# One forward step of a hybrid backbone: another order of instructions in the odd layer

## The chip, the cores and the metric

The kernel runs on one core of one Trainium2 chip. The time is device microseconds of an execution, as the median of several runs. The chip's engines are TensorE (PE), VectorE (DVE), ScalarE (ACT), GpSimd (POOL) and SyncE (SP), which here issues all DMAs. Each engine runs its own instructions in the order in which they were written, and waits on semaphores where one needs another's result.

## The reference, cut to what matters

Two groups of tokens (128 context tokens and 256 latent tokens, each 1024 wide) go through two layers. Layer 0 has a Fourier mixer and attention as its mixer, layer 1 (the odd layer) an RG-LRU and a bidirectional Mamba-2 SSD. A SwiGLU network follows each mixer. All is float32. The mixer of the odd layer, shortened:

```python
p = h @ w_in
g, xl, z, xbc, dt = split(p)
xc = centred_dwconv(xl)                       # RG-LRU, 4 tiles of 128 channels
y_lru = (scan_forward(xc) + scan_backward(xc)) * gelu(g)
xs, B, C = split(silu(centred_dwconv(xbc)))   # SSD: 16 heads of 64
acs = cumsum(dt * A)                          # per direction, chunks of 128
decay = exp(where(causal, acs_q - acs_k, -inf))
y = sum_k (C_q . B_k) * decay * dt_k * xs_k + C_q * exp(acs_q) @ state_in
y_ssd = rmsnorm((y_forward + y_backward + d * xs) * silu(z))
out = concat(y_lru, y_ssd) @ w_out
```

## The kernel before, in words

Activations stand with channels on the partitions and 386 columns: 128 context tokens, two extra columns for the modulation, 256 latent tokens. Weights come in blocks of 128 by 128, eight to a DMA of 512 KB (tile `wr`). ScalarE and VectorE split each chunk into a high and a low part (`wh`, `wl`), the activations likewise (`xh`, `xl`; `mh`, `ml`; `gh`, `gl`), and `mm3` (L620) adds three products for each block. A tile of 128 outputs is so 24 products of 386 columns for the input projection, in one of 8 PSUM banks (tag `ps`).

`odd_mixer` (L1108) runs over 27 such tiles in the order of `names` (L1111): dt0 bc0 bc1 z0 xs0 z1 together, then xs1 xs2 z2 z3 xs3 xl0 z4 xs4 xs5 xl1 z5 xl2 xs6 xs7 xl3 z6 z7 g0 g1 g2 g3. What is done with a tile is recorded right behind it. `xs_tile` (L1337) convolves, transposes and weighs two heads' channels; after every second xs tile `states` (L1367) makes state products and `ssd` (L1388) is recorded twice, for two heads each. So there are four stages of four heads, behind xs1, xs3, xs5 and xs7. For a head `ssd` does the following:

- for each direction d, in rows 64d to 64d + 63: one product of 384 columns (`ps<-rr,pick`) and three of 128 columns (`ps<-pick,rr`) in a bank of the direction's own;
- a product with the identity over all rows (`ps<-mask,identr`) that adds the causal mask, then Exp on ScalarE into a tile `M`; VectorE adds the two directions and multiplies by C.B;
- one product of 64 rows for the incoming states (`ps<-ee,sel`), which VectorE multiplies into `exs`;
- for the two heads of a call together, the output in one bank, each head in 64 of the array's columns (`ps<-M,xt`, `ps<-exs,Hc`).

The shapes of array that a product takes are called forms here: (rows, columns), each rounded up to 32, 64 or 128. A projection or mask product has the form (128, 128), the directions' products (64, 128), head outputs and state products (128, 64).

No engine's order is written by hand. `Recorder.add` (L230) notes every operation with its place `seq` in the program, its dependences and the buffers that it takes. `Recorder.schedule` (L307) then plans them one by one against a model of the engines' times and emits them in the order of their planned starts. For each engine it looks at the ready operations, takes the earliest start, and among those that can start by then the one with the lowest place. For TensorE, `quarter` holds when each part of the array is free; a product can start when the parts of its `groups` are. How the model decides depends on which part of the program holds the oldest open operation: 0 the first mixer, 1 its SwiGLU, 2 `odd_mixer`, 3 the second SwiGLU. `PARTS` (L213) has six numbers for each:

1. `window`: an operation that takes a buffer may be this many places ahead of the oldest open one;
2. `keep` and 3. `close`: of the 70 SBUF slots (tag `s`), an operation `gap` places ahead must leave more than min(1, gap / close) x keep free (L362);
4. `pad`: microseconds added between another engine's result and the TensorE operation that uses it (L449);
5. `hold`: background loads give way to other work that starts within this time;
6. `forms`: None, or the number of places by which a TensorE operation of another form than the last is put back. With a number, operations that can start within 2 x 0.105 us of the first are compared, and a change of form waits until all parts of the array are free, and `DRAIN` (0.105 us) more (L369 to L389).

Of the kernel before, what the change touches and what calls it, by code (L numbers as in the profile page):

```python
# [181 lines left out]
def meet(a, b):  # L182
    return all(x[0] < y[1] and y[0] < x[1] for x, y in zip(a, b))
# [16 lines left out]
class Recorder:  # L200
# [12 lines left out]
    PARTS = (  # L213
        (900, 10, 150, 0.8, 0.25, 60),
        (500, 12, 150, 0.4, 0.15, None),
        (900, 6, 120, 0.8, 0.25, None),
        (500, 12, 150, 0.4, 0.15, None),
    )

# [10 lines left out]
    def add(self, eng, cost, outs, ins, fn, func=None, tail=0.0, cols=0.0):  # L230
        o = Op()
        o.seq, o.eng, o.cost, o.fn, o.func, o.tail = len(self.ops), eng, cost, fn, func, tail
        o.prio = o.seq + self.base
        o.far = self.base >= self.FAR
        o.chain, o.part = self.chain, self.part
        o.cols, o.groups = cols, (0, 1, 2, 3)
        if eng == "PE":
            a, b = outs[0].box[0]
            o.groups = range(a // 32, -(-b // 32))
            k, n = ins[0].shape[0], outs[0].shape[0]  # L240
            o.form = tuple(32 if v <= 32 else 64 if v <= 64 else 128 for v in (k, n))
        if o.chain is not None:
            o.chain[0] += 1
        deps = {}
        tiles = set()
        o.allocs = []
        for v in ins:
            if not isinstance(v, Vw):
                continue
            t = v.t  # L250
            tiles.add(t)
            assert t.live, t.name
            for w, box in t.writes:
                if t.psum or meet(box, v.box):
                    deps[w] = True
            if t.psum:

                for r, box in t.reads:
                    if r.eng != eng:
                        deps[r] = True  # L260
            t.reads.append((o, v.box))
        for v in outs:
            if not isinstance(v, Vw):
                continue
            t = v.t
            tiles.add(t)
            if not t.live:
                t.live = True
                t.first = None
                if t.tag is None:  # L270
                    self.fixed.append(t)
                else:
                    t.first = o
                    o.allocs.append(t)
            elif t.first is not None and t.first is not o:
                deps[t.first] = True
            for w, box in t.writes:
                if t.psum or meet(box, v.box):
                    deps[w] = True
            keep = []  # L280
            for r, box in t.reads:
                if r is not o and (t.psum or meet(box, v.box)):
                    deps[r] = True
                else:
                    keep.append((r, box))
            t.reads = keep
            inside = lambda b: all(y[0] <= x[0] and x[1] <= y[1] for x, y in zip(b, v.box))
            t.writes = [(w, b) for w, b in t.writes if not (w is not o and inside(b))] if not t.psum else []
            t.writes.append((o, v.box))
        if o.far and eng == "SP" and self.after is not None:  # L290
            deps[self.after] = True
        if self.gate is not None:
            deps[self.gate] = True
        deps.pop(o, None)
        o.deps = list(deps)
        o.users = []
        for d in o.deps:
            d.users.append(o)
        o.n = len(o.deps)
        o.est = 0.0  # L300
        o.tiles = tiles
        for t in tiles:
            t.left += 1
        self.ops.append(o)
        return o

    def schedule(self):  # L307
# [6 lines left out]
        table = [None]  # L314
        dma_free = [0.0]

        ticks, quarter = {}, [0.0] * 4
        form = [None]
        order = []

        def avail(o):

            t = 0.0
            need = {}
            for a in o.allocs:
                if a.tag is not None:
                    need[a.tag] = need.get(a.tag, 0) + 1
            for tag, n in need.items():
                s = slots[tag]
                if len(s) < n:  # L330
                    return None
                t = max(t, heapq.nsmallest(n, s)[-1])
            return t
# [15 lines left out]
        while left:  # L349
# [5 lines left out]
            for e in engines:  # L355
                cand = []
                for o in ready[e]:
# [7 lines left out]
                    a = avail(o) if o.allocs else 0.0  # L365
                    if a is None:
                        continue
                    if e == "PE":
                        if forms is None or o.form == form[0]:  # L369
                            a = max(a, *(quarter[g] for g in o.groups))  # L370
                        else:
                            a = max(a, max(quarter) + self.DRAIN)
# [3 lines left out]
                    if e == "SP":  # L376

                        a = max(a, dma_free[0] - self.AHEAD)
# [21 lines left out]
            _, s, o = best  # L400
# [11 lines left out]
            else:  # L412
                if e == "PE":
# [3 lines left out]
                    while todo > 1e-9:  # L417
                        i = int(now / self.TICK + 1e-9)
                        c = cost if ticks.get(i - 1, 0.0) >= 3060 else 2 * cost
# [1288 lines left out]
```

## Time and profile before

| What | Before |
|---|---|
| median of 3 runs | 1012.6 us (1011.65 to 1015.13) |
| profiled execution | 1011.14 us, its span 1009.4 us |
| mean granted TensorE clock | 0.976 of full |
| busy: PE, PEld, DVE, ACT, POOL | 985.2, 932.4, 733.7, 503.4, 4.3 us |
| DMA queue q1 | 158.84 MB, 45.1% of 16 engines' span |
| stretch of the odd mixer after its first tiles | 494 to about 754 us (it holds the next SwiGLU's first products too) |

Times in the rows are microseconds from the start of the span. PE is TensorE's matmuls, PEld its weight loads. `ps<-xh,wh` is a product into PSUM of operands xh and wh; 64*128 after MATMUL are the rows and columns of the array that it uses, 64x384 the moving operand. PEclk is the clock that TensorE was granted, as a share of 2.4 GHz; an instruction's name with x6 stands for six in a row. An interval in square brackets is idle time before an instruction and what ended it. A float32 product that isn't split takes two instructions.

### The profile page before, as it was taken

Reading aid. Unit: us, or ns where it says so; the run is one execution under the profiler, and the core shown is the slowest. Engines: PE = TensorE matmul, PEld = TensorE weight load, DVE = VectorE, ACT = ScalarE, POOL = GpSimd, SP = SyncE. Lnnn points to the kernel's source line nnn. Section 1 sums busy time; section 2 is a strip of 40 time slices with the busy share of each in tenths; the row PEclk is TensorE's granted clock in tenths of the full one; section 3 lists DMA queues with packets and bytes.
Section 4 is the critical chain, followed back from the end, with each engine's and each line's share of the span. In section 5 each row is a group of like instructions: output and inputs, shape, how many; then the busy total and the mean of one; then the engine's idle time right before and its main releaser. Section 6 shows DMA issues by size and latency. Waiting matters only on the chain.

```text
span 1009.4 us, 16165 instructions
## 1 busy us (share of the span) xinstructions
PE 985.2 (98%) x6190; PEld 932.4 (92%) x6190; DVE 733.7 (73%) x1550; ACT 503.4 (50%) x951; POOL 4.3 (0%) x41
## 2 busy tenths in 40 slices
PE   6999999999999999999999899999999999999998
PEld 4987889999999999999977778899999999999998
DVE  4589666999999999984696778776889555553342
ACT  4578866343333433443496759673635333333221
POOL 0000000000000000000000000000000000000000
PEclk9999999999999999999996979899999999999999
DMA  9983426755666668643220112133463333333340
GB/s 359 368 307 110 150 85 221 256 188 196 225 213 223 215 229 259 209 148 129 89 84 11 63 47 84 48 114 130 155 251 124 125 119 120 120 122 127 125 163 24
DMA packets 47179, 159.85 MB, mean 158 GB/s; under 512 B 5376, under 2 KB 9216, under 8 KB 47104
## 3 DMA queue, kind: packets, MB, share of 16 engines
q1 hardware_dynamic: 47104, 158.84, 45.1%
q8 instruction: 48, 0.79, 0.3%
q14 instruction: 27, 0.22, 0.1%
HBM read 156.45 MB, written 2.37 MB: 157 GB/s over the span
## 4 chain that ended last, share of the span: by engine, by line
PE 91%; ACT 5%; DMA 2%; issue 1%; DVE 1%; SPq 0%; DVEq 0%; ACTq 0%
PE ps L588 89%; DMA ar<-in_ada 2%; PE ps L592 2%; ACT L528 1%; ACT kk L528 1%; SPq L581 0%; ACT ex L528 0%; ACT kl L528 0%; ACT qq L528 0%; ACT wh L528 0%; ACT M L528 0%; ACT pT L528 0%; ACT t L528 0%; ACT th L528 0%; ACT rstd L528 0%
## 5 line engine op out<-in xcount | busy, mean ns | idle before, releaser
L528 ACT ACTIVATE wh<-wr 128x1024 fp32r<-128x1024 f32 x191 | 202.0, 1058 | 360.1 <-PE ps L588 249.4
L588 PE MATMUL ps<-xh,wh 128*128 128x386 f32 x1016 | 349.5, 345 | 2.2 <-ACT rstd L528 2.2
L588 PE MATMUL ps<-xl,wh 128*128 128x386 f32 x1016 | 349.4, 344 | 0.0
L588 PE MATMUL ps<-xh,wl 128*128 128x386 f32 x1016 | 347.4, 342 | 0.0
L538 DVE TENSOR_TENSOR wl<-wr,wh 128x1024 fp32r<-128x1024 f32 x191 | 233.2, 1221 | 111.6 <-ACT wh L528 108.1
L588 PEld LDWEIGHTS ps<-xh,wh 128*128 128x128 f32 x1016 | 193.4, 191 | 6.3 <-ACT rstd L528 2.8
L588 PEld LDWEIGHTS ps<-xl,wh 128*128 128x128 f32 x1016 | 193.4, 190 | 4.2 <-issue 3.4
L588 PEld LDWEIGHTS ps<-xh,wl 128*128 128x128 f32 x1016 | 193.7, 191 | 0.9 <-issue 0.5
L551 DVE SCALAR_TENSOR_TENSOR junk<-ar,scb 128x1024 bf16<-128x1024 f32 x112 | 136.5, 1219 | 2.8 <-DMA ar<-in_ada 2.2
L588 PE MATMUL ps<-gl,wh 128*128 128x384 f32 x352 | 118.6, 337 | 0.0
L588 PE MATMUL ps<-gh,wl 128*128 128x384 f32 x352 | 118.6, 337 | 0.0
L588 PE MATMUL ps<-gh,wh 128*128 128x384 f32 x352 | 118.6, 337 | 0.0
L538 DVE TENSOR_TENSOR ft<-ps,rstd 128x386 f32<-128x386 f32 x88 | 48.3, 558 | 53.0 <-PE ps L588 50.9
L588 PEld LDWEIGHTS ps<-gl,wh 128*128 128x128 f32 x352 | 66.2, 188 | 0.0
L588 PEld LDWEIGHTS ps<-gh,wl 128*128 128x128 f32 x352 | 66.1, 188 | 0.0
L588 PEld LDWEIGHTS ps<-gh,wh 128*128 128x128 f32 x352 | 66.1, 188 | 0.0
L588 PE MATMUL ps<-ml,wh 128*128 128x384 f32 x160 | 54.3, 339 | 0.0
L588 PE MATMUL ps<-mh,wh 128*128 128x384 f32 x160 | 54.2, 339 | 0.0
L588 PE MATMUL ps<-mh,wl 128*128 128x384 f32 x160 | 53.3, 337 | 0.0
L528 ACT ACTIVATE xh<-x,G 128x128 fp32r<-128x128 f32 x64 | 26.3, 445 | 23.7 <-DVE x L551 16.7
L551 DVE SCALAR_TENSOR_TENSOR fs<-ft,fs 128x128 f32<-128x128 f32 x88 | 33.3, 414 | 4.0 <-ACT wh L528 0.5
L528 ACT ACTIVATE gh<-fs 128x384 fp32r<-128x384 f32 x44 | 23.1, 525 | 26.2 <-DVE fs L551 26.0
(226 smaller groups left out, 1082.5 us busy)
## 6 DMA issues: line engine op xcount, KB each, us to landing
wr<-in_wst SPq DMA_DIRECT2D x191, 512.0 KB, 3.3
ar<-in_ada SPq DMA_DIRECT2D x96, 512.0 KB, 4.7
x<-in_x SPq DMA_DIRECT2D x4, 386.0 KB, 9.7
out_y<-x SPq DMA_DIRECT2D x8, 193.0 KB, 2.8
scb<-in_cond SPq DMA_DIRECT2D x2, 512.0 KB, 6.6
lw<-in_lru_w SPq DMA_DIRECT2D x2, 512.0 KB, 4.6
Hc<-in_h SPq DMA_DIRECT2D x2, 256.0 KB, 4.8
out_new_ssd<-news SPq DMA_DIRECT2D x4, 128.0 KB, 1.8
```

The source lines that it names most:

```text
L528: lambda: nc.scalar.activation(out=R(out), in_=R(in_), func=func, bias=R(bias), scale=R(scale), accum_out=R(accum_out)),
L538: self.dve(out, [a, b], out.free, lambda: nc.vector.tensor_tensor(out=R(out), in0=R(a), in1=R(b), op=op))
L551: lambda: nc.vector.scalar_tensor_tensor(out=R(out), in0=R(a), scalar=R(s), in1=R(b), op0=op0, op1=op1, accum_out=R(accum_out)),
L588: self.rec.add("PE", c / 1e3, [out], [lhsT, rhs], lambda: nc.tensor.matmul(R(out), R(lhsT), R(rhs), start=start, stop=stop), cols=cols)
L592: self.rec.add("PE", 0.109, [out], [in_, ident], lambda: nc.tensor.transpose(R(out), R(in_), R(ident)), cols=2 * in_.shape[0])
```

## The change

Three places. The numbers of part 2 become (900, 10, 150, 0.4, 0.25, 200): ten slots held back with a distance of 150 instead of six with 120, a pad of 0.4 us instead of 0.8, and forms weighed with 200 places instead of not at all. The model of the array has 16 groups, four of rows by four of columns, where it had four of columns; a product takes those of the rows of its stationary operand and the columns of its output. No operation is added, removed or altered; buffers and their numbers are the same.

```diff
     PARTS = (
         (900, 10, 150, 0.8, 0.25, 60),
         (500, 12, 150, 0.4, 0.15, None),
-        (900, 6, 120, 0.8, 0.25, None),
+        (900, 10, 150, 0.4, 0.25, 200),
         (500, 12, 150, 0.4, 0.15, None),
     )
...
-        o.cols, o.groups = cols, (0, 1, 2, 3)
+        o.cols, o.groups = cols, range(16)
         if eng == "PE":
             a, b = outs[0].box[0]
-            o.groups = range(a // 32, -(-b // 32))
+            c, d = ins[0].box[0]
+            o.groups = [r * 4 + g for r in range(c // 32, -(-d // 32)) for g in range(a // 32, -(-b // 32))]
             k, n = ins[0].shape[0], outs[0].shape[0]
...
-        ticks, quarter = {}, [0.0] * 4
+        ticks, quarter = {}, [0.0] * 16
```

## Rows read from the trace of the kernel before

**Rows 1.** The page: busy time by engine, and the chain that ended last.
```profile
PE 985.2 (98%) x6190; PEld 932.4 (92%) x6190; DVE 733.7 (73%) x1550; ACT 503.4 (50%) x951; POOL 4.3 (0%) x41
...
PE 91%; ACT 5%; DMA 2%; issue 1%; DVE 1%; SPq 0%; DVEq 0%; ACTq 0%
```

**Rows 2.** Table of stretches: length, busy time by engine, PEclk, DMA share, GB/s.
```profile
528.22:545.29 17.07, 16.77 (x82) 11.51 (x83) 10.24 (x27) 9.62 (x25) 0.00 (x0) 0.50 0.02 8
...
552.11:555.53 3.42, 3.42 (x11) 3.07 (x10) 3.39 (x8) 1.99 (x6) 0.00 (x0) 0.50 0.00 0
...
579.42:593.07 13.65, 12.73 (x45) 8.31 (x45) 12.18 (x32) 8.67 (x20) 0.00 (x0) 0.50 0.11 40
593.07:627.20 34.13, 34.13 (x193) 29.20 (x192) 24.13 (x53) 27.17 (x49) 0.00 (x0) 1.00 0.24 81
627.20:637.44 10.24, 10.24 (x43) 7.63 (x41) 9.60 (x26) 9.43 (x24) 0.10 (x1) 0.50 0.00 1
```

**Rows 3.** Table of stretches, of instructions on xh alone: PE, PEld, DVE, ACT.
```profile
522.70:551.90 29.20, 0.00 (x0) 0.00 (x0) 0.00 (x0) 0.00 (x0) 0.71 0.03 10
...
572.70:587.00 14.30, 0.13 (x1) 0.00 (x0) 0.00 (x0) 0.00 (x0) 0.73 0.10 37
...
617.90:631.70 13.80, 0.10 (x2) 0.01 (x1) 0.25 (x4) 0.00 (x0) 0.84 0.22 77
```

**Rows 4.** Timeline of PE around head outputs: start, length, instruction.
```profile
640.91 0.34 PE L588 MATMUL ps<-xh,wl 128*128 128x386 f32 x1
641.08 0.34 PE L588 MATMUL ps<-xh,wh 128*128 128x386 f32 x1
641.36 0.44 PE L588 MATMUL ps<-exs,Hc 128*64 128x128 f32 x4
641.62 0.39 PE L588 MATMUL ps<-M,xt 128*64 128x128 f32 x4
641.84 0.61 PE L588 MATMUL ps<-exs,Hc 128*64 128x128 f32 x8
...
642.50 0.39 PE L588 MATMUL ps<-exs,Hc 128*64 128x128 f32 x4
642.82 0.44 PE L588 MATMUL ps<-xl,wh 128*128 128x386 f32 x1
643.10 0.34 PE L588 MATMUL ps<-xh,wl 128*128 128x386 f32 x1
```

**Rows 5.** Timeline of PE, a head of the third stage.
```profile
572.76 0.45 PE L588 MATMUL ps<-rr,pick 64*128 64x384 f32 x2
573.04 0.45 PE L588 MATMUL ps<-pick,rr 64*128 64x128 f32 x6
573.42 0.61 PE L588 MATMUL ps<-mask,identr 128*128 128x384 f32 x2
573.96 0.38 PE L588 MATMUL ps<-ee,sel 64*128 64x256 f32 x1
```

**Rows 6.** Timeline of PE, a head of the fourth stage.
```profile
622.79 0.33 PE L588 MATMUL ps<-rr,pick 64*128 64x384 f32 x1
...
623.33 0.44 PE L588 MATMUL ps<-mask,identr 128*128 128x384 f32 x1
623.70 0.44 PE L588 MATMUL ps<-rr,pick 64*128 64x384 f32 x1
...
624.72 0.38 PE L588 MATMUL ps<-ee,sel 64*128 64x256 f32 x1
```

**Rows 7.** Waits of PE from 494 to 754: total, times, longest us.
```profile
PE ps L588 <- DVE cv L551: 2.0, 1, 2.0
...
PE ps L588 <- ACT M L528: 0.3, 1, 0.3
```

**Rows 8.** Table of stretches, most of the odd mixer.
```profile
493.00:680.00 187.00, 180.28 (x1000) 151.90 (x998) 147.07 (x348) 140.58 (x277) 0.24 (x3) 0.88 0.18 63
```

**Rows 9.** Timeline of PE, third stage, idle time in brackets.
```profile
579.59 0.69 PE L588 MATMUL ps<-M,xt 128*64 128x128 f32 x2 [2.04 <-DVE cv L551]
```

## The prediction, on record before the run

> **What bounds the kernel now.** Read the page first: TensorE is busy 98% of the span, and its matmuls fill 91% of the chain that ended last [rows 1]. Nothing else has to be made faster; the question is how many of its busy microseconds are needed. The table of stretches answers that. The odd layer's mixer is where the small products of the SSD stand, and there TensorE is busy at the lower of its two clock levels: the granted clock is 0.50, which is 1.2 of 2.4 GHz, from 528.22 to 545.29, 579.42 to 593.07 and 627.20 to 637.44, and in one short stretch of 3.42 us at 552.11 [rows 2]. That is 17.07 + 13.65 + 10.24 + 3.42 = 44.4 us, and TensorE is busy in nearly all of it (16.77 of 17.07, 12.73 of 13.65, 10.24 of 10.24). Between 593.07 and 627.20 the granted clock is 1.00.
>
> Next comes what TensorE did in those places. Restricted to the products of the input projection, which fill the array (xh and xl against wh and wl), the table shows none from 522.7 to 551.9, one from 572.7 to 587.0 and two from 617.9 to 631.7 [rows 3]. Each stretch begins with small SSD products at full clock, and the clock falls while they go on without full-array work; once such work is back it rises. The SSD comes in four stages of four heads (after xs1, xs3, xs5, xs7); the first two run as one block from 519 to 552, the third from 572.8, the fourth from 617.9. In these the order takes the oldest ready operation, and the SSD is older than the next projection tiles, so these stay behind.
>
> The timeline gives the price of changing the tile form. Full-array products follow one another every 0.17 to 0.18 us; with a change to the 64-column form the step is 641.36 - 641.08 = 0.28, the four products before the change back take 642.82 - 642.50 = 0.32 where four took 641.84 - 641.62 = 0.22, and the first full product after it 643.10 - 642.82 = 0.28 [rows 4]. A change and back costs some 0.30 us, 0.15 for each. From 494 to 754 I count 94 changes, the last that at 642.82; 47 belong to the first two stages, 23 to the third, 24 to the fourth.
>
> Then the heads. In the third stage a head's two directions, in rows 0 to 63 and rows 64 to 127, run at once: its eight products and two masks take 573.96 - 572.76 = 1.20 us [rows 5]. In the fourth, a full-array mask stands between the directions, and the same head takes 624.72 - 622.79 = 1.93 us [rows 6], both at full clock. Waits are the smallest item: eight, from 2.0 down to 0.3, 6.7 us together [rows 7].
>
> **The change part by part.** It issues the same instructions; only their order moves, on every engine, and only from the point where the oldest open operation is in the odd mixer. In the first part nothing can move: its products use all 128 rows, except some that use rows 0 to 63 (or 0 to 95) and have no partner in the others, so 16 groups say what 4 said.
>
> Forms weighed, 200 places. While TensorE is in the full form, an SSD operation is now taken only if it is over 200 places older than the next projection product. Counted from the code, four heads are 88 operations, so when stage 3 is ready the next tile (xl1) is 91 places younger, and in stage 4 (xl3) also 91; a tile without a convolution is 28 places and one with it 49. So two to four tiles, 48 to 96 products, now come ahead of or between the heads of stages 3 and 4, and each bunch of heads lets as many more follow. That is the mix that stood at 1.00 from 593.07 to 627.20 [rows 2]. Of the 13.65 + 10.24 = 23.9 us at 1.2 GHz in those stages I let two thirds, 16 us, go; work that took 16 takes 8: **-8 us**. The first block I leave as it is: when it starts, the next tile is 343 or more places younger than its oldest head, beyond 200. Bounds: all 44.4 us go (-22), or one more stretch as long as stage 3's appears (+6.8), if bunches of equal form are themselves long enough to lower the clock.
>
> Here a rule speaks against the change. In the trace VectorE is busy 12.18 of the 13.65 us of stage 3's slow stretch and 9.60 of 10.24 in stage 4's [rows 2]; if the heads' eviction and masking set the pace there, a faster array gains 1.5 + 0.6 us. The Trainium skill, TensorEngine Tiling (Array Packing), section Performance Considerations, says that packing speeds up the array but not the copying out of PSUM, which may then be the bottleneck. By it the first term would be -2.1 instead of -8. I keep -8, because from 493 to 680 VectorE is busy 147 of 187 us [rows 8]: spread over the whole stage its work leaves room, and what fills the array meanwhile is projection.
>
> Fewer changes of form. Staying in a form takes two heads' 64-row products together, as far as the eight PSUM banks allow, and leaves masks to follow together. I take 94 to 60, 34 x 0.15 = **-5 us**. Bounds: two per head, 32 (-9), and, if banks run out after each half head, 110 (+2.4).
>
> Sixteen groups. The order now knows that rows 64 to 127 are free while the others work, so the second direction is put right behind the first. Of the 1.93 - 1.20 = 0.73 us that a split head loses, two changes of form (0.30) are in the term above; 0.43 is overlap. Stage 4's four heads: 4 x 0.43 = **-1.7**. Bounds: eight heads (-3.4), or heads paired now that are split for want of a bank, as many the other way (+3.4).
>
> Margin 0.8 to 0.4. A result of ScalarE or VectorE is expected 0.4 us sooner by TensorE, so its product stands earlier in a queue that runs in order; everything behind it waits with it, projection too. The largest such wait is 2.04 us, which the profile puts down to a convolution; it ended at 579.59, and the clock fell at 579.42, while it lasted [rows 2, 7, 9]. More tiles at hand should hide some waits and the thinner margin open others: I take **+2**. Bounds: the present 6.7 vanish (-6.7), or each of some 30 hand-offs of the mixer (8 transposes, 4 states, 8 head outputs, 4 gates, 6 others) comes the whole 0.4 late (+12).
>
> Ten slots held back instead of six, of 70. An operation far ahead that needs a slot waits longer; then its PSUM bank stays taken and the next tile cannot start. What hides it is the 200 places: no tile gets further ahead than that while heads are ready. I take 0; at worst it takes back the 8 us of the first term, and since fewer held tiles could also unblock an older head, at best one long wait goes (-2). Weight loads move with the tiles; the DMA engines are busy 0.18 of this stretch [rows 8], so they are there in time.
>
> Sum: -8 - 5 - 1.7 + 2 = -12.7. The profiled execution took 1011.1 us (span 1009.4 and 1.7 around it): 998.4. The median of the runs is 1.5 above it: **999.9 us**.
>
> **Rivals.**
> *No change (0.15).* The 200 places hardly bind, or the heads' evictions set the pace: the first term is -2.1, pairing nothing, 14 changes fewer (-2.1), margin +4: about 0, 1012.6. For it: VectorE's share in the slow stretches, and the page's rule above, which has its chance here. Against it: the 30 us block without projection, in which VectorE is busy 10.24 of 17.07, has room.
> *Slower by late hand-offs (0.20).* Place: head outputs and transposes in stages 3 and 4. All 30 hand-offs 0.4 late cost 12 and cancel the gains of 14.7 nearly; and as after the 2.04 us wait [rows 9], a slow stretch such as 13.65 us follows in a stage, 6.8 more. Sum -14.7 + 12 + 6.8 = +4: 1017. It decides from 0.3 us late per hand-off on, with one such stretch. For it: all eight waits of now are on results of VectorE or ScalarE. Against: the two later stages have much more independent work between.
> *Much faster (0.15).* The first block mixes as well, because stage 2's heads are only 142 places older than tile z4: the clock term is -20, forms -6.5: 1011.1 - 26.5 + 1.5 = 986.
>
> **How the numbers follow.** The forecast, 994 to 1007, gets 0.50. What the measurement can tell from no change is 0.3%, 3 us. Faster: 0.50 + 0.15 = 0.65; same 0.15; slower 0.20. The range reaches down to the much faster case and up to just under the slower one's middle: 986 to 1016.
>
> **What would show it.** Right: granted clock 1.00 in most of stages 3 and 4, projection products inside them, some 60 changes of form, no split head, the first block still slow at its start. Wrong in the first term: the slow stretches stay about 44 us although projection stands between. Wrong in the margin: waits on VectorE and ScalarE in the mixer well over 9 us. What would make the whole prediction wrong is a longer stretch of slow clock behind new waits, or projection tiles stopped for want of banks.

## The result, and the profile after

The kernel after the change takes 982.13 us (median of four executions, 981.72 to 983.47); the kernel before took 1012.12 beside it (1009.89 to 1015.13). The ratio is 0.9704, with an interval of 0.9677 to 0.9731: 30 us faster, where 12.7 were forecast, and below the low end of my range.

First the page: busy time by engine, the granted clock in 40 slices, and the chain that ended last.

```profile
PE 958.7 (98%) x6190; PEld 916.9 (94%) x6190; DVE 731.0 (75%) x1550; ACT 499.4 (51%) x949; POOL 4.3 (0%) x41
...
PEclk9999999999999999999999999899999999999999
...
PE 87%; ACT 8%; DVE 2%; issue 1%; DMA 1%; SPq 0%; DVEq 0%; ACTq 0%
```

TensorE is still what bounds the kernel, at 98%; it is busy 26.5 us less with the same 6190 products [rows 1]. Next the table of stretches (length, busy time of PE, PEld, DVE, ACT and POOL, granted clock, DMA share, GB/s).

```profile
493.00:680.00 187.00, 182.71 (x1162) 164.96 (x1162) 161.29 (x372) 147.15 (x292) 0.10 (x1) 0.98 0.24 82
...
524.40:534.60 10.20, 9.89 (x85) 7.08 (x86) 10.08 (x26) 6.28 (x18) 0.00 (x0) 1.00 0.04 13
614.20:621.03 6.83, 6.83 (x30) 4.37 (x30) 5.02 (x16) 4.47 (x15) 0.10 (x1) 0.50 0.18 68
573.00:587.00 14.00, 13.53 (x90) 10.69 (x89) 12.29 (x30) 10.21 (x18) 0.00 (x0) 1.00 0.30 97
```

In the same 187 us TensorE now issues 1162 products where it issued 1000, at a mean clock of 0.98 in place of 0.88 [rows 8]. Of the 44.4 us at 1.2 GHz [rows 2] one stretch of 6.83 us is left. The table for the instructions on `xh` alone, which stand for the projection, shows what I had looked for and what I had not:

```profile
524.40:534.60 10.20, 0.00 (x0) 0.15 (x1) 0.00 (x0) 0.00 (x0) 1.00 0.04 13
...
572.00:587.00 15.00, 8.05 (x29) 5.05 (x29) 0.00 (x0) 0.00 (x0) 1.00 0.29 91
```

In the third stage projection stands between the heads, 29 products where one stood [rows 3]. But in the first block there are 10.2 us of the heads' products without any projection, and they run at 1.00. The timeline of PE at that block's start (start, length, instruction, idle time in brackets) and PE's waits from 494 to 740 (total, times, longest):

```profile
518.47 1.14 PE L589 MATMUL ps<-mask,identr 128*128 128x384 f32 x5
519.45 0.34 PE L589 MATMUL ps<-xh,wh 128*128 128x386 f32 x1
...
521.77 0.44 PE L589 MATMUL ps<-rr,pick 64*128 64x384 f32 x1 [1.10 <-ACT et L529]
```
```profile
PE ps L589 <- ACT rstd L529: 1.5, 2, 0.7
PE ps L589 <- ACT et L529: 1.1, 1, 1.1
PE ps L589 <- DVE exs L539: 0.7, 1, 0.7
...
PE ps L593 <- DVE ysum L552: 0.2, 1, 0.2
```

Masks follow one another (five) and a projection tile comes between heads already here. The waits sum to 5.0 us after 6.7 [rows 7]. Changes of the tile form fall from 94 to 42, by my count.

So the profiled execution's 1011.14 - 981.94 = 29.2 us divide as follows, by estimate. Clock: (1 - 0.976) x 1009.4 = 24.2 us lost before, (1 - 0.994) x 980.2 = 5.9 after, 18.3 gained. Changes of form: 52 x 0.15 = 7.8, at the prediction's price, which no run measures by itself. Waits 1.7. The remaining 1.4 is not assigned.

### The profile page after: what moved, and what is told of

Read it like the earlier page. It is cut to its first block, busy times and chain, and to the rows that moved or that the text cites. A ratio compares the mean times of both kernels' runs of the same rounds, so it can differ in the third digit from the quotient of the medians.

```text
span 980.2 us, 16154 instructions
## 1 busy us (share of the span) xinstructions
PE 958.7 (98%) x6190; PEld 916.9 (94%) x6190; DVE 731.0 (75%) x1550; ACT 499.4 (51%) x949; POOL 4.3 (0%) x41
## 4 chain that ended last, share of the span: by engine, by line
PE 87%; ACT 8%; DVE 2%; issue 1%; DMA 1%; SPq 0%; DVEq 0%; ACTq 0%
PE ps L589 85%; PE ps L593 2%; ACT wh L529 1%; DMA ar<-in_ada 1%; ACT L529 1%; ACT xw L529 1%; ACT kk L529 1%; ACT X L529 1%; ACT M L529 0%; SPq L582 0%; ACT cv L529 0%; ACT ex L529 0%; ACT kl L529 0%; ACT th L529 0%; ACT xt L529 0%
## 5 line engine op out<-in xcount | busy, mean ns | idle before, releaser
L529 ACT ACTIVATE xh<-x,G 128x128 fp32r<-128x128 f32 x64 | 26.3, 446 | 23.9 <-DVE x L552 16.8
```

Of the source, the lines that this page charges most:

```text
L529: lambda: nc.scalar.activation(out=R(out), in_=R(in_), func=func, bias=R(bias), scale=R(scale), accum_out=R(accum_out)),
```

## The experiments

Four edits came together, so each is run alone on the kernel before (e1 to e4), and left out alone from the kernel after (e5 to e8). The others test mechanisms. "Slow clock" is the time at 1.2 GHz in the odd mixer, with changes of form (490 to 760) and PE waits (494 to 740, us), all from the profiled execution. That can be a lucky one: e2's is the fastest of its five. So the last column gives the mean granted clock of every execution, lowest to highest (before: of the 53 beside the experiments).

| Run | Median us | Ratio to before, interval | Slow clock | Changes | Waits | Clocks |
|---|---|---|---|---|---|---|
| before | 1012.1 | | 44.4 | 94 | 6.7 | 0.970 to 0.985 |
| after | 982.1 | 0.9677 to 0.9731 | 6.8 | 42 | 5.0 | 0.991 to 0.994 |
| e1 weighing alone | 996.9 | 0.9819 to 0.9905 | 30.7 | 33 | 11.6 | 0.984 to 0.988 |
| e2 sixteen groups alone | 997.8 | 0.9825 to 0.9926 | 10.2 | 71 | 8.7 | 0.981 to 0.992 |
| e3 margin alone | 1004.5 | 0.9903 to 0.9955 | 41.0 | 82 | 5.2 | 0.978 to 0.986 |
| e4 slots alone | 1013.4 | 0.9993 to 1.0041 | 44.4 | 100 | 6.3 | 0.971 to 0.983 |
| e5 all but groups | 998.0 | 0.9821 to 0.9877 | 23.9 | 33 | 14.0 | 0.984 to 0.989 |
| e6 all but weighing | 980.8 | 0.9669 to 0.9708 | 3.4 | 76 | 1.9 | 0.996 to 0.998 |
| e7 all but margin | 985.0 | 0.9711 to 0.9755 | 6.8 | 40 | 7.0 | 0.991 to 0.995 |
| e8 all but slots | 981.3 | 0.9663 to 0.9723 | 0 | 40 | 4.8 | 0.993 to 0.998 |
| e9 after, no side by side | 982.6 | 0.9691 to 0.9758 | 0 | 42 | 2.0 | 0.991 to 1.000 |
| e10 before, no side by side | 1013.7 | 1.0010 to 1.0041 | 51.2 | 94 | 3.4 | 0.971 to 0.976 |
| e11 groups and margin 0.4 | 979.9 | 0.9671 to 0.9714 | 3.4 | 76 | 1.9 | 0.995 to 0.998 |
| e12 e6, margin in part 0 | 984.7 | 0.9717 to 0.9755 | 0 | 76 | 2.5 | 0.998 to 1.000 |
| e13 before, cost not doubled | 1000.2 | 0.9843 to 0.9886 | 27.3 | 103 | 2.9 | 0.983 to 0.988 |
| e14 before, sums copied early | 997.8 | 0.9826 to 0.9863 | 23.9 | 96 | 2.5 | 0.984 to 0.988 |
| e15 after, late `et` | 983.6 | 0.9685 to 0.9719 | 3.4 | 42 | 6.7 | 0.993 to 0.995 |
| e16 e11, sums copied early | 995.0 | 0.9779 to 0.9845 | 27.3 | 72 | 7.8 | 0.982 to 0.991 |
| e17 e11 with margin 0.3 | 982.6 | 0.9682 to 0.9725 | 0 | 83 | 3.1 | 0.997 to 1.000 |
| e18 e11 with margin 0.5 | 985.1 | 0.9716 to 0.9749 | 3.4 | 81 | 4.1 | 0.995 to 0.997 |

### One edit alone

```diff
-        (900, 6, 120, 0.8, 0.25, None),
+        (900, 6, 120, 0.8, 0.25, 200),     # e1
+        (900, 6, 120, 0.4, 0.25, None),    # e3
+        (900, 10, 150, 0.8, 0.25, None),   # e4
...
-        o.cols, o.groups = cols, (0, 1, 2, 3)
+        o.cols, o.groups = cols, range(16) # e2, with the lines of the change that belong to it
```

> Forms weighed with 200 places in the odd layer, all else as before. Theory A (the weighing mixes projection into the heads and lets the clock stay up; it carries most of the 30 us): 986 to 994 us, slow clock in the odd mixer under 15 us of the former 44, about 30 changes of form. Theory B (the 16 groups carry it, by packing the two directions): 1003 to 1011, slow clock 30 us or more. Theory C (only the four numbers together do it): within 5 us of before.

> 16 groups, all else as before. Theory A: 1004 to 1011 us (some split heads joined, fewer changes, slow clock still 30 us or more). Theory B: 985 to 995 us, slow clock under 15 us. Theory C: within 5 us of before.

> Margin 0.4 instead of 0.8 us in the odd layer, all else as before. Theory A: 1008 to 1016 us; waits of TensorE in the odd mixer 6 to 12 us, slow clock about 44 us. If the margin itself were what kept TensorE from its work, 1000 to 1006 us.

> Ten slots held back with distance 150 instead of six with 120, all else as before. Theory A: 1009 to 1016 us, no gain by itself. If slots taken early were what held older heads back, 1000 to 1007 us.

Weighing and the groups each gain some 15 us alone, the margin 7.6, the slots nothing. None of the three theories is right: 996.9 and 997.8 lie between the ranges of A and B, and each edit alone gives about half of the gain. The margin, at 1004.5, falls where it was itself what kept TensorE from its work. The table of stretches, of e1 first and then of e2:

```profile
523.12:536.77 13.65, 12.76 (x61) 10.51 (x59) 11.76 (x29) 9.28 (x26) 0.00 (x0) 0.50 0.03 10
574.32:581.15 6.83, 6.74 (x25) 6.31 (x26) 6.69 (x16) 5.05 (x13) 0.00 (x0) 0.50 0.14 54
625.52:635.76 10.24, 7.90 (x24) 6.04 (x25) 8.27 (x23) 7.68 (x19) 0.00 (x0) 0.50 0.16 53
```
```profile
521.00:541.00 20.00, 18.41 (x147) 13.39 (x147) 18.41 (x44) 15.89 (x42) 0.14 (x2) 1.00 0.17 54
568.38:575.21 6.83, 6.81 (x27) 6.50 (x28) 5.12 (x13) 5.01 (x14) 0.00 (x0) 0.50 0.23 78
```

With weighing alone, the edit on which I had put the clock, all three places keep a slow stretch, 30.7 us together. It has 61 changes of form fewer (some 9 us) and 13.7 us less at 1.2 GHz (some 7), and waits 4.9 us more. With the groups alone the first block runs at 1.00 in the execution that was profiled. But the five executions of e2 differ by the clock: 991.61 us at 0.992 (the profiled one), 996.88 and 997.78 at 0.986, 999.33 at 0.983, 1000.85 at 0.981. Counted over all executions, as the time multiplied by the share that is missing from full clock, the median loss by this estimate is 25.3 us before, 15.5 with weighing alone and 14.0 with the groups alone. Alone, the two give back about the same of the clock, and neither gives back all.

### All but one edit

Here each of the lines above is undone in the kernel after, one in each kernel.

> All of the change but the 16 groups (four groups as before). Theory B2 (the groups keep the clock up, because both directions of a head and neighbouring heads are put side by side; the weighing only saves changes of form): 990 to 1000 us, 25 us or more of slow clock in the odd mixer, about 30 changes. Theory A (the weighing and the projection between the heads keep the clock up): 982 to 988, slow clock under 12 us.

> All of the change but the weighing of forms (None in the odd layer). Theory B2: 986 to 993 us, slow clock under 14 us, about 70 changes, so that what is missing is 5 to 8 us of changes. Theory A: 998 to 1008 us, slow clock 30 us or more.

> All of the change but the margin (0.8 us as before). If the 7.6 us that the margin alone gained add to the rest: 987 to 992 us. If it gained only what the groups and the forms gain too (fewer changes): 980 to 985 us.

> All of the change but the slots (six held back, distance 120). As ten alone gained nothing: 980 to 985 us. If the weighing needs the ten, because products run ahead and their evictions take the slots: 988 us or more, with new waits of TensorE on VectorE or ScalarE.

Only the groups are clearly missed: without them the gain is halved, with 23.9 us of slow clock and waits of 14.0. Without the margin 2.8 us are lost (e7), with an interval that overlaps that of after. PE's waits of e5, the two longest:

```profile
PE ps L588 <- DVE exs L538: 3.9, 2, 2.0
PE ps L588 <- ACT et L528: 2.0, 1, 2.0
```

Weighing, worth 15 us alone, is worth nothing on top of the rest: e6 without it is as fast as after, faster than both theories allowed (A, which gave the clock to the weighing, is out by e5 as well), with 76 changes of form in place of 42. Those 34 changes, some 5 us, are balanced by waits (5.0 against 1.9) and clock (6.8 against 3.4). The table of stretches of e6, then the same for `xh` alone, then its waits:

```profile
527.00:545.00 18.00, 17.98 (x173) 13.36 (x172) 16.61 (x41) 15.30 (x40) 0.00 (x0) 1.00 0.05 15
...
493.00:680.00 187.00, 185.73 (x1169) 166.45 (x1168) 162.51 (x376) 148.28 (x295) 0.23 (x3) 0.99 0.25 83
```
```profile
527.00:545.00 18.00, 0.00 (x0) 0.00 (x0) 0.00 (x0) 0.00 (x0) 1.00 0.05 15
```
```profile
PE ps L589 <- ACT rstd L529: 1.5, 2, 0.7
PE ps L589 <- ACT et L529: 0.4, 1, 0.4
```

For 18 us e6 issues no projection product (none on `xl` either), at full clock: 173 products, where before issued 82 in 17.07 us at half the clock [rows 2]. That refutes the premise of my first term, that heads without projection between them lower the clock. The two stretches don't hold the same mixture, though: e6 has 12 masks and 13 of the 384-wide direction products among its 173, before 4 and 3 among its 82. Masks fill the array as projection does, so e6 is not free of full-array work, and no run shows whether the mixture matters.

### Is it the array's two halves at work at once?

The groups let the order put a head's two directions side by side. Theory B2 says that this is what keeps the clock up; its rival, that the order does. e9 keeps the order of after, and e10 that of before, but the 64-row products of both directions are issued in rows 0 to 63, so that they can't run at once; the planner still sees the old rows.

```diff
-                    self.mm(q[d][:, :NC_], r, S["rr"][ds], True, False)
+                    z = slice(0, 64)
+                    r0 = S["pick"][z, d * 16 + h:d * 16 + h + 1].to_broadcast([64, 128])
+                    self.mm(q[d][:, :NC_], r, S["rr"][ds], True, False, (r0, S["rr"][z]))
...
-                        self.mm(q[d][:, cc], S["nrr"][ds, cc], r, False, False)
+                        self.mm(q[d][:, cc], S["nrr"][ds, cc], r, False, False, (S["nrr"][z, cc], r0))
```

> The changed kernel in its own order, instruction for instruction, but the products of both directions of a head use rows 0 to 63 (those rows hold a copy of the same data), so that no two of them can run at once. Theory B2 (both directions side by side in the array are what keeps the clock up): slow clock in the odd mixer 25 us or more, 997 to 1008 us. Rival (the clock is kept by the order alone, fewer waits and denser queues; side by side saves only its overlap of 16 heads x 0.33 us): 984 to 990 us, slow clock under 14 us.

> The kernel before in its own order, with both directions in rows 0 to 63. Theory B2: some heads of before did run side by side, so it loses, 1015 to 1022 us, slow clock 45 us or more. Rival: about 7 heads x 0.33 to 0.66 us, 1014 to 1017 us. If before had nothing from it: within 2 us of before.

The timeline of PE in e9 shows a head one after the other, then the table of stretches and its longest wait:

```profile
530.64 0.61 PE L590 MATMUL ps<-rr,pick 64*128 64x384 f32 x2
531.10 0.77 PE L590 MATMUL ps<-pick,rr 64*128 64x128 f32 x6
```
```profile
493.00:680.00 187.00, 185.33 (x1165) 170.31 (x1166) 161.80 (x375) 146.82 (x292) 0.10 (x1) 1.00 0.25 82
```
```profile
PE ps L590 <- ACT et L529: 0.8, 1, 0.8
```

Two products take 0.61 and six 0.77 where both took 0.45 side by side [rows 5], and yet e9 is as fast as after, in the profiled execution at 1.00 throughout. So theory B2 falls: running at once is not what keeps the clock up, and in the medians it gains nothing. In after's profile the time saved stands against more waits (5.0, in e9 2.0) and more slow clock (6.8, in e9 none). At the same clock it does gain: at 0.994 and 0.991 e9 took 983.75 and 988.09 us, after 981.94 and 983.47. What the groups bring beyond these 2 to 5 us is the order that the planner makes of them. e10, with the order of before, is 1.8 us slower than before (1013.7 against 1011.9 beside it). Its 51.2 us of slow clock are what B2 forecast, but its clocks, 0.971 to 0.976, lie within those of before, so it decides nothing.

### The best pair, and its neighbours

e11 takes groups and margin alone; e12 is e6 with the margin 0.4 in part 0 too, the first layer's mixer; e17 and e18 move e11's margin by 0.1.

```diff
         (900, 10, 150, 0.8, 0.25, 60),     # part 0: 0.4 in e12
...
-        (900, 6, 120, 0.8, 0.25, None),
+        (900, 6, 120, 0.4, 0.25, None),    # e11; 0.3 in e17, 0.5 in e18
```

> 16 groups and the margin of 0.4 us, slots and forms as before. Groups alone gave 997.8 us, groups with margin and slots 980.8. If the margin is what the groups need (products offered sooner, so that the array is filled without gaps): 979 to 984 us, slow clock under 8 us, some 70 changes, waits under 4 us. If the slots are needed beside it: 988 us or more.

> Search for a better version: 16 groups, margin 0.4 and ten slots in the odd layer, no weighing there, and the margin of 0.4 us in the first part too (0.8 so far). The first 150 us have 15 us in which TensorE waits or a chain runs through ScalarE, so 970 to 981 us if the thinner margin fills them, 981 to 986 if results come late there.

> Sixteen groups in the array's model, and a margin of 0.3 us in place of 0.4 in the odd layer; slots and forms as before. Theory M (sixteen groups with a margin well under 0.8 us give an order that keeps TensorE fed, and so the clock): 978 to 985 us, slow clock in the odd mixer under 8 us, as with 0.4. Rival L (0.4 was one lucky order among many, and any neighbouring number draws a new one): 985 to 1000 us here or with 0.5, with 10 to 30 us at 1.2 GHz.

> Sixteen groups, and a margin of 0.5 us in the odd layer; slots and forms as before. Theory M: 978 to 986 us, slow clock under 8 us. Rival L: 985 to 1000 us here or with 0.3.

e11 is the fastest median, 979.87 us, though its interval overlaps that of after. e12 is no better version: it lost 4 us to e6 with the odd mixer at full clock. Part of that is lost ahead of the mixer: up to 494 us it has issued 3341 products, e6 3353, though its waits there are no longer. The neighbours lie 2.8 and 5.3 us above e11, and both run the same 18 us at 1.00, with a little projection in them, as the table of stretches shows, of e17 and then of e18, each with its `xh` products alone behind it:

```profile
527.00:545.00 18.00, 18.00 (x153) 13.21 (x151) 16.95 (x41) 12.18 (x33) 0.00 (x0) 1.00 0.03 8
527.00:545.00 18.00, 3.46 (x12) 1.86 (x10) 0.00 (x0) 0.00 (x0) 1.00 0.03 8
```
```profile
527.00:545.00 18.00, 18.00 (x159) 12.84 (x158) 16.13 (x39) 13.23 (x35) 0.00 (x0) 1.00 0.05 15
527.00:545.00 18.00, 1.31 (x4) 0.57 (x3) 0.00 (x0) 0.00 (x0) 1.00 0.05 15
```

So 0.4 was no single lucky order: with groups, margins of 0.3 to 0.5 give 980 to 985, and 0.8 gives 998 (e2).

### Is it the planner's belief, or a wait?

Theory P says that the planner makes slow stretches because it believes in them, theory W that a long wait for `et` at the block's start brings the clock down. e13 lets before's planner never double a product's cost in the odd layer, as it does where it expects the slow clock. e14 and e16 copy the sums `tot` out of PSUM on VectorE ahead of the exponential `et`, on before and on e11; e15 makes after wait longer for `et`, whose exponential is done six times.

```diff
-                        c = cost if ... else 2 * cost
+                        c = cost if self.ops[front[0]].part == 2 or ... else 2 * cost   # e13
...
+            totc = self.tile("totc", 96, F32, "c")                # e14, e16
+            self.ts(totc, tot[:, 0:96], 0.0, ALU.add)
+            self.act(et, totc, AF.Exp)
...
+            one = self.rec.ops[-1].fn                             # e15
+            self.rec.ops[-1].fn = lambda: [one() for _ in range(6)]
```

> The kernel before (four groups, its own four numbers), with one line of the planning altered: in the odd layer its model never doubles a product's cost, so the plan does not count on a slow clock there. Theory P (with four groups the plan takes the two directions for one after the other, counts on the slow clock, and lays ScalarE's and VectorE's work for a slow TensorE; the 16 groups helped by this alone): 985 to 1000 us, slow clock in the odd mixer under 20 us. Rival (the places of the products themselves, which only the groups change): 1005 to 1016 us, slow clock 30 us or more.

> The kernel before, with the sums of dt x A copied out of PSUM by VectorE, so that the bank is free without ScalarE's late Exp: the wait of 1.3 us on it before the first heads goes. Theory W (that wait starts the fall of the clock in the first block: in the runs so far the clock fell within 4 us of it wherever it was 1.3 us or more, but for two kernels, and nowhere where it was 1.1 or less): 998 to 1004 us, slow clock in the first block under 8 us. Rival (the wait only coincides): 1008 to 1013 us, slow clock there 14 us or more.

> The changed kernel in its own order, with that Exp done six times over, so that it comes some 1 us later and TensorE's wait before the first heads grows from 1.1 to about 2 us. Theory W: the clock falls near 522 and stays low for 7 us or more; 986 to 991 us. Rival: only the wait itself, 982.5 to 985 us, no fall there.

> Search for a better version: 16 groups and the margin of 0.4 us, slots and forms as before (979.9 us), and the copy out of PSUM of the run without the wait. The wait is 0.4 us there already: 977 to 981 us. Every theory expects that; a loss would mean that the order elsewhere got worse.

The tables of stretches of e13, e14, e16 and e15, in that order:

```profile
524.31:537.96 13.65, 13.65 (x52) 8.84 (x51) 7.86 (x20) 7.78 (x18) 0.00 (x0) 0.50 0.00 0
613.05:626.70 13.65, 13.65 (x43) 11.13 (x43) 10.26 (x28) 9.51 (x25) 0.00 (x0) 0.50 0.07 27
```
```profile
523.67:533.91 10.24, 10.24 (x42) 6.86 (x42) 7.09 (x18) 5.64 (x15) 0.00 (x0) 0.50 0.00 0
...
612.42:622.66 10.24, 10.24 (x42) 7.31 (x42) 10.22 (x29) 10.16 (x27) 0.00 (x0) 0.50 0.02 6
```
```profile
521.94:532.18 10.24, 10.13 (x43) 7.16 (x43) 6.64 (x16) 7.99 (x19) 0.00 (x0) 0.50 0.10 34
569.73:579.97 10.24, 8.60 (x47) 7.66 (x48) 8.77 (x24) 9.76 (x21) 0.00 (x0) 0.50 0.00 1
```
```profile
524.81:528.22 3.41, 3.41 (x14) 2.93 (x12) 3.06 (x8) 3.41 (x11) 0.00 (x0) 0.50 0.01 2
```

And the waits of e15 and of e16:

```profile
PE ps L589 <- ACT et L529: 2.5, 1, 2.5
```
```profile
PE ps L589 <- ACT M L529: 3.7, 2, 3.5
PE ps L589 <- ACT th L529: 2.6, 1, 2.6
...
PE ps L589 <- ACT er L529: 0.4, 1, 0.4
```

As the cause of the long stretches theory W falls. e14 and e16 have no wait for `et`, and the clock falls at the block's start all the same, for 10.24 us; ahead of it e16's longest wait in that block is the one of 0.4 us on `er`. (The time of e14, 997.8, is the one that W forecast, but not for W's reason.) e15 more than doubles the wait, to 2.5 us. The clock does fall behind it, at 524.81, where after has no slow stretch, but for 3.41 us instead of 7 or more, and the time is that of after. So a long wait may bring a short fall; that rests on one execution. Theory P holds in part at most: e13 gains 14 us, and 27.3 us of slow clock stay. e14 and e16 carry the same edit: it gains 16 us on before and loses 15 on e11. It changes the order of the whole mixer, and the new order has its own clock and waits.

What stays open is which property of an order lets the clock fall. Over all executions, ten of the twelve programs with sixteen groups have clocks of 0.991 or more, and all eight without stay at 0.989 or less; e2 and e16, with groups, come down to 0.981 and 0.982. Projection between heads, the two halves at once and waits alone don't decide it: some falls come at the end of a long wait (in e2 at 568.38, with a wait of 2.66 us until 568.40; in before at 579.42, with 2.04 us until 579.59 [rows 9]), others without any, as that at 627.20 before, behind 34.13 us of unbroken work [rows 2]. The mixture of the products is not tested.

## Why the prediction was wrong

The direction was right, and so was the bound: TensorE's time is the kernel's time. Point by point:

- **Forms weighed, -8.** The step that failed, in two places. I credited the clock to this edit and "the first block I leave as it is"; the clock gained 18.3 us, in the first block too, and weighing is not needed for it: e6 and e11 reach 0.995 or more without it. Needed are the groups (e5, without them, loses 14.0 us to the clock in the median), and with them the thinner margin or the weighing (e11 2.9 us, e7 5.9, the groups alone 14.0). My premise, read from stretches that held both projection and full clock [rows 2, 3], took what stood together for a cause. The trace of before spoke against it already: the clock rose at 545.29, while projection was away until 551.9 [rows 3], and fell again at 552.11, just as it was back. The stretch between the two slow ones, from the table of stretches of before:

```profile
545.29:552.11 6.82, 6.21 (x40) 4.26 (x36) 3.79 (x9) 5.93 (x14) 0.00 (x0) 1.00 0.07 22
```

- **Fewer changes, -5.** The direction held: 42 in place of 60, or -7.8 by the same price, still an estimate. But e6, with 76, is as fast as after.
- **Sixteen groups, -1.7.** The largest error. I priced them by the overlap of a head's directions, and that overlap is worth nothing in the medians and 2 to 5 us at equal clock (e9). As an input of the planner they decide the order: leaving them out costs 15.9 us (e5).
- **Margin, +2.** The sign was wrong: alone -7.6, and with the groups 997.8 to 979.9. Its waits went down, from 6.7 to 5.2 alone and from 8.7 to 1.9 with the groups, where I expected late hand-offs. With weighing in place it matters less (e7: 985.0).
- **Slots, 0.** Right (e4, e8).

Of the rivals, no change by VectorE's evictions fell: VectorE is busy 161.29 us of the 187 and TensorE still gained. The Trainium skill, TensorEngine Tiling (Array Packing), section Performance Considerations, warns that copying out of PSUM may become the bottleneck. The first block of after comes close to it: from 524.4 to 534.6 VectorE is busy 10.08 of 10.20 us, but TensorE is busy 9.89 of them too. Late hand-offs did not come in after, but they did where the waits of TensorE grew: 11.6 us in e1, 8.7 in e2, 14.0 in e5, 7.8 in e16. The much faster rival, 986, came nearest, by luck in part: the first block mixes at its start, as it said, but e6 shows that the mixing is not needed and that the gain is not that of weighing.

## What to carry to other kernels

Price an edit of a planner's model by the order that comes out, not by the hardware effect that it describes: the same edit gained 16 us on one base and lost 15 on another. Where several such edits come together, run each alone and leave each out alone: weighing gained 15 us alone and nothing beside the others. And count the time at the lower clock first, over all executions and not in the profiled one alone: among these programs it was the largest single difference.

## What the runs showed of the hardware

A product of TensorE in other rows of the array can start ahead of products that stand before it in the program. The program of before issues a head of the third stage as one 384-wide and three 128-wide products in rows 0 to 63 and then the same four in rows 64 to 127; in the trace the two wide ones start at 572.758 and 572.771, and the six others follow from 573.04 on [rows 5]. So the order of writing, to which the beginning of this text holds each engine, does not bind these starts. The Trainium skill, TensorE: Matmul & The Clock Gate, section The mechanism, says that matmuls keep the program's order in start and end; by these starts they do not across rows.

The clock stayed at 1.2 GHz with TensorE never idle in the stretch, 13.65 of 13.65 us twice in e13, and it fell behind unbroken work: at 627.20 before, where TensorE had been busy for all of the 34.13 us ahead [rows 2]. And one program's executions differ by it: those of e2 lie 9.2 us apart.
